# Eight blocks of a projection as one Strassen group of 512 + 512 columns, with PSUM in four pairs of banks

## The chip, the cores and the metric

The kernel runs on one core of one Trainium2 chip. The metric is the device time of one execution in microseconds, as the median of several runs; lower is better.

## What is computed

One layer of a hybrid bidirectional encoder on 512 tokens of width 2048, all in float32. The part that matters here is the input projection: h = RMSNorm(x), proj = h @ w_in, with w_in of 2048 x 10752. Its columns are cut into q, k, v and gate of a differential attention (branch A, eight heads), q, k, v and gate of a grouped-query attention with rotary positions (branch B), and two merge gates of 2048 columns.

```python
h = rmsnorm(x, norm_g)
proj = einsum('bsd,dc->bsc', h, w_in)
qa, ka, va, za, qb, kb, vb, zb, ga, gb = split(proj)
oa = diff_attention(...)                 # branch A, heads of 128
ya = (rmsnorm(oa) * 0.8 * silu(za)) @ w_out_a
ob = gqa_attention(axial_rope(rmsnorm(qb)), axial_rope(rmsnorm(kb)), vb)
yb = (ob * silu(zb)) @ w_out_b
out = rmsnorm(x + (sigmoid(ga) * ya + sigmoid(gb) * yb) @ w_o, final_g)
```

## The kernel before

**Arithmetic.** Each float32 operand of a matmul is split into a high part in fp32r (a cast on ScalarE, L103) and a low part (a subtraction on VectorE, L104). A product is three matmuls: high x high, low x high, high x low. The activations are split once; weights are split as they stream (split_w, L113), into tiles w_hi and w_lo of the pool wp, which has three buffers of each, 4 KB a partition each, and lives through the whole kernel.

**Columns and groups.** The projection is cut into blocks of 128 columns. Blocks 0, 1, 8, 9 stream plainly at the start (plain_rows). STRASSEN_BLOCKS then lists four groups of four blocks: 16 to 19, 20 to 23, 24 to 27 and 28 to 31 (in the text: groups 0 to 3). They are the values of branch A (16 to 23), keys and values of branch B (24 to 27) and queries of branch B (28 to 31). Twelve Strassen groups for the gates follow, and then the attention heads, with the rest of the projection as filler between them.

**A Strassen group (strassen, L186).** Activations are four quarters of 256 tokens x 1024 rows of the sum: a11, a12, a21, a22, and the sums s1 to s4, all held split. The weights of a group are four quarters of 1024 rows x 256 columns: b11, b12 (upper rows, left and right columns), b21, b22. Seven products of 256 x 256 x 1024 are made in the order p1 (a11 b11), p2 (a12 b21), p5 (s1), p6 (s2), p3 (s3), p4 (s4), p7 (a22). Between them VectorE makes the weight sums in place (sub, L209: b11 = b12 - b11, b11 = b22 - b11, b12 = b22 - b12, b21 = b21 - b11) and the output sums (plus, L240, and kept, L432). One product is 2 token blocks x 8 row blocks x 3 = 48 matmuls of 256 columns at L234, into one PSUM bank. For groups 0 to 3 x is the stationary operand and w moves; for the gates it is the other way round.

**Raw weights.** Eight slots w_raw of 4 KB a partition (slots, raw_tile) hold the four quarters, two slots each. After a group the list slots is rotated so that the next group takes them in the order in which they came free. Loads are issued on SP's queue.

**Results.** In group 0 the sums land in slices of xt and are stored to pv in DRAM by keep_cols, one DMA per block of 128 columns (L303). From group 1 on they land in tiles kept of the pool sp (six buffers of 2 KB) and are stored the same way.

**Pools.** Pools of tiles are opened and closed in the code; in SBUF they are stacked in the order of their opening, and a pool opened after others have closed takes their place. Over const, wraw, wp and xa (the split activations) lies xs (s1 to s4, 64 KB). Over xs lies first xn (grow 0.5 KB, xt 32 KB, two tiles early of 2 KB and some small ones), which closes after group 0, and then sp. After the gates sp and xs close, and the heads' pools at (first tile: cols) and atc (ca, sa, tables) take their place. PSUM is one pool of eight banks: four (acc) go round among the products, four (aux) are used at the start and by the heads.

**Order.** TensorE keeps the order of the program here. The instructions of VectorE, ScalarE and SP are put in order by a planner that goes by the program's order and by when an instruction can start; it also puts in the waits. Each engine then works its own list in order.

Of the kernel before, what the change touches and what calls it, by code (L numbers as in the profile page):

```python
# [11 lines left out]
F32 = mybir.dt.float32  # L12
F32R = mybir.dt.float32r
AF = mybir.ActivationFunctionType
ALU = mybir.AluOpType
AX = mybir.AxisListType

P = 128
D = 2048
S = 512  # L20
NT = S // P
NK = D // P
# [13 lines left out]
    for i in range(n)  # L36
}

STRASSEN_BLOCKS = [(16, 17, 18, 19), (20, 21, 22, 23), (24, 25, 26, 27), (28, 29, 30, 31)]
FILL_BLOCKS = [(32, 33), (2, 10), (3, 11), (34, 35), (4, 12), (5, 13), (6, 14), (7, 15)]  # L40
HEADS = "B0 B1 A0 B2 B3 B4 B5 A1 A2 B6 B7 A3 A4 A5 A6 A7".split()

# [7 lines left out]
def hybrid_block_kernel(  # L50
# [8 lines left out]
    nc = tc.nc  # L59
# [1 line left out]
    const = ctx.enter_context(tc.tile_pool(name="const", bufs=1))  # L61
    dram = ctx.enter_context(tc.tile_pool(name="dram", bufs=1, space=bass.MemoryType.DRAM))

    ps_pool = ctx.enter_context(tc.tile_pool(name="ps", bufs=1, space=bass.MemoryType.PSUM))
    banks = {}

    def share_banks(**kw):
        banks.update(kw)

    def bank(kind, shape):  # L70
        ring = banks[kind]
        ring.append(ring.pop(0))
        return ps_pool.tile([P, *shape], F32, name=kind, tag=f"bank{ring[-1]}")

    def acc_tile(*shape):
        return bank("acc", shape)
# [2 lines left out]
        return bank("aux", shape or (S,))  # L79

    wraw = ctx.enter_context(tc.tile_pool(name="wraw", bufs=1))
    wp = ctx.enter_context(tc.tile_pool(name="wp", bufs=3))

    ident = const.tile([P, P], F32, name="ident")
    make_identity(nc, ident)
# [21 lines left out]
    slots = [f"w_raw{i}" for i in range(8)]  # L107
    turn = [0]

    def raw_tile(slot, shape, dtype=F32):  # L110
        return wraw.tile([P, *shape], dtype, name="w_raw", tag=slots[slot])

    def split_w(raw, free=None):  # L113

        shape = list(raw.shape)
        if free is None:
            hi = wp.tile(shape, F32R, name="w_hi", tag="w_hi")
            lo = wp.tile(shape, F32R, name="w_lo", tag="w_lo")
        else:
            hi, lo = (raw_tile(free + i, shape[1:], F32R) for i in range(2))  # L120
        hi_lo(hi, lo, raw)
        return hi, lo
# [63 lines left out]
    def strassen(w, c_left, c_right, act, natural, tmp, done, tail=None, before={}):  # L186
# [89 lines left out]
        o = [slots[2 * i:2 * i + 2] for i in range(4)]  # L276
        slots[:] = o[1] + o[0] + o[3] + o[2]

    zg = dram.tile([2 * BW, S], F32, name="zg")
    gg = dram.tile([2 * D, S], F32, name="gg")  # L280
    og = dram.tile([2 * BW, S], F32, name="og")
# [17 lines left out]
    def keep_cols(blocks, t0, nt, v):  # L299

        for i, b in enumerate(blocks):
            written[b] = written.get(b, 0) + nt
            nc.sync.dma_start(out=pv[b, :, t0:t0 + nt, :], in_=v[:, :, i * P:(i + 1) * P])  # L303
# [21 lines left out]
    def plain_rows(blocks, place, **kw):  # L325
# [9 lines left out]

        return stream_steps(w_in, column_pieces(blocks), NK, False, act, kept, **kw)

    share_banks(acc=[0, 1, 2, 3], aux=[4, 5, 6, 7])
    with tc.tile_pool(name="xs", bufs=1) as xs:


        for n in ("s1", "s2", "s3"):
# [2 lines left out]
        with tc.tile_pool(name="xn", bufs=1) as xn:  # L345
# [106 lines left out]

            project(STRASSEN_BLOCKS[0], early, in_xt, before={"s2": late_sums})

        with tc.tile_pool(name="sp", bufs=6) as sp:
            def tmp():
                return sp.tile([P, 2, 256], F32, name="kept", tag="kept")

            for blocks in STRASSEN_BLOCKS[1:]:
                project(blocks, tmp, lambda ps: tmp())  # L460


            nc.sync.dma_start(out=sub_g, in_=subln_g.rearrange("o p -> p o"))
            nc.vector.tensor_scalar(out=sub_g, in0=sub_g, scalar1=LAM_INIT - 1.0, scalar2=None, op0=ALU.mult)
            lam4, lprod = (sp.tile([P, n, 64], F32, name="lam", tag="kept") for n in (4, 2))
            for i, v in enumerate((lq1, lk1, lq2, lk2)):
                nc.sync.dma_start(out=lam4[:, i, :], in_=v.broadcast_to([P, 64]))
            for i in range(2):
                nc.vector.tensor_tensor(out=lprod[:, i, :], in0=lam4[:, 2 * i, :], in1=lam4[:, 2 * i + 1, :], op=ALU.mult)
            nc.vector.tensor_reduce(out=lsum, in_=lprod, axis=AX.X, op=ALU.add)  # L470
            nc.scalar.activation(out=lsum, in_=lsum, func=AF.Exp)
            nc.vector.tensor_tensor(out=nlam, in0=lsum[:, 1:2], in1=lsum[:, 0:1], op=ALU.subtract)
            nc.vector.tensor_scalar(out=nlam, in0=nlam, scalar1=-LAM_INIT, scalar2=None, op0=ALU.add)


            for c0, n, func, dst in ((O_ZA, BW, AF.Silu, zg[0:BW]), (O_ZB, BW, AF.Silu, zg[BW:]),
                                     (O_GA, D, AF.Sigmoid, gg[0:D]), (O_GB, D, AF.Sigmoid, gg[D:])):
                for g in range(0, n, S):
                    def gate(th, ch, ps, sb, g=g, func=func, dst=dst):
                        v = tmp()  # L480
                        nc.vector.tensor_tensor(out=v, in0=ps, in1=sb, op=ALU.add)
                        nc.scalar.activation(out=v, in_=v, func=func)
                        row = g + ch * 256
                        nc.sync.dma_start(
                            out=dst[row:row + 256, th * 256:th * 256 + 256].rearrange("(c p) t -> p c t", p=P),
                            in_=v)

                    strassen(w_in, c0 + g, c0 + g + 256, xq, False, tmp, gate)


    share_banks(acc=[4, 5], aux=[6, 7, 0, 1, 2, 3])


# [592 lines left out]
```

## Time and profile before

| | |
|---|---|
| median of 3 runs | 1378.22 us (1376.71 to 1378.24) |
| the profiled execution | 1376.67 us |
| its span, first to last instruction | 1374.9 us |
| TensorE busy (matmuls) | 1350.2 us, 98% of the span |
| VectorE busy | 1081.1 us, 79% |
| ScalarE busy | 702.9 us, 51% |
| HBM | 144 GB/s over the span |

The predicted time is to be compared with the median; single numbers of a stage come from the profiled execution, in microseconds from the start of its span. Groups 0 to 3 run from 69.21 to 230.49, the gates after them. A matmul's end is modelled and matmuls are pipelined, so the distance between starts tells what one costs, not its duration. In the rows, L234 is the line of kernel.py, PE is TensorE, DVE VectorE, ACT ScalarE, POOL GpSimd, SP SyncE; PEld is the weight load; a q behind an engine means its queue of DMA issues.

### The profile page before, as it was taken

The numbers are of one execution on the slowest core, as the hardware profiler recorded it, in microseconds if no ns is written. First come the engines' busy times: TensorE is split into PE (matmuls) and PEld (weight loads), VectorE is DVE, ScalarE is ACT, GpSimd is POOL, SyncE is SP. The second block draws the span as 40 slices with busy tenths as digits, with TensorE's granted clock in tenths as the row PEclk, the third lists the DMA queues.
The fourth block names the chain that finished last, engine by engine and source line by source line (L and its number), as shares of the span: only waits on it lengthen the run. The fifth ranks groups of instructions, "written<-read, shape, count | busy, mean of one in ns | idle before, by whom it ended". The sixth has DMA issues, their size and how long they took to land.

```text
span 1374.9 us, 24100 instructions
## 1 busy us (share of the span) xinstructions
PE 1350.2 (98%) x9625; PEld 1274.1 (93%) x9625; DVE 1081.1 (79%) x1400; ACT 702.9 (51%) x1110; POOL 84.5 (6%) x94
## 2 busy tenths in 40 slices
PE   6999999999999999999999999999999999999997
PEld 6999999999999999999998888888788888899997
DVE  5977787777777777777759778787898858899886
ACT  7643333444444444444446675575676753354444
POOL 1000000000000000000003201000000010004322
PEclk9999999999999999999999999999999999999999
DMA  8245434543333444333377454545575446463333
GB/s 291 77 147 161 124 116 149 154 146 113 118 121 123 148 149 143 117 122 118 123 207 220 122 154 147 153 139 162 171 221 182 130 145 202 151 245 116 97 95 123
DMA packets 201743, 204.21 MB, mean 149 GB/s; under 512 B 11280, under 2 KB 175392, under 8 KB 200992
## 3 DMA queue, kind: packets, MB, share of 16 engines
q1 hardware_dynamic: 201632, 202.69, 47.5%
q8 instruction: 75, 1.23, 0.4%
q14 instruction: 36, 0.29, 0.1%
HBM read 165.68 MB, written 32.77 MB: 144 GB/s over the span
## 4 chain that ended last, share of the span: by engine, by line
PE 90%; DVE 4%; ACT 2%; DMA 1%; issue 1%; POOL 0%; SPq 0%; DVEq 0%; POOLq 0%; ACTq 0%
PE acc L234 55%; PE acc L175 27%; PE aux L621 3%; PE aux L608 2%; PE aux L739 1%; DVE w_lo L104 1%; PE aux L664 1%; PE aux L665 1%; DVE w_raw L209 1%; DMA rows<-og 1%; DMA xt<-in_x_dram 1%; PE aux L389 0%; DMA rows<-yg 0%; ACT sq L366 0%; ACT w_hi L103 0%
## 5 line engine op out<-in xcount | busy, mean ns | idle before, releaser
L103 ACT CAST w_hi<-w_raw 128x1024 fp32r<-128x1024 f32 x351 | 368.5, 1050 | 516.8 <-PE acc L234 397.9
L104 DVE TENSOR_TENSOR w_lo<-w_raw,w_hi 128x1024 fp32r<-128x1024 f32 x351 | 431.9, 1232 | 168.7 <-ACT w_hi L103 168.2
L209 DVE TENSOR_TENSOR w_raw<-w_raw 128x1024 f32<-128x1024 f32 x160 | 200.0, 1250 | 2.4
L234 PE MATMUL acc<-a2h,w_hi 128*128 128x256 f32 x384 | 108.7, 283 | 0.0
L234 PE MATMUL acc<-a2l,w_hi 128*128 128x256 f32 x384 | 108.7, 283 | 0.0
L234 PE MATMUL acc<-a2h,w_lo 128*128 128x256 f32 x384 | 108.7, 283 | 0.0
L234 PEld LDWEIGHTS acc<-a2h,w_hi 128*128 128x128 f32 x384 | 73.7, 192 | 0.0
L234 PEld LDWEIGHTS acc<-a2l,w_hi 128*128 128x128 f32 x384 | 73.7, 192 | 0.0
L234 PEld LDWEIGHTS acc<-a2h,w_lo 128*128 128x128 f32 x384 | 73.7, 192 | 0.0
L576 DVE TENSOR_REDUCE nmax<-aux 128x1 f32<-128x512 f32 x96 | 61.0, 681 | 7.5 <-PE aux L739 4.7
L175 PE MATMUL acc<-a1h,w_hi 128*128 128x512 f32 (+1 forms) x160 | 56.6, 358 | 0.2 <-ACT a1h L393 0.2
L175 PE MATMUL acc<-a1l,w_hi 128*128 128x512 f32 (+1 forms) x160 | 55.6, 353 | 0.1
L175 PE MATMUL acc<-a1h,w_lo 128*128 128x512 f32 (+1 forms) x160 | 55.7, 353 | 0.0
L175 PE MATMUL acc<-a2l,w_hi 128*128 128x512 f32 (+1 forms) x160 | 55.5, 348 | 0.0
L175 PE MATMUL acc<-a2h,w_hi 128*128 128x512 f32 (+1 forms) x160 | 55.5, 350 | 0.0
L175 PE MATMUL acc<-a2h,w_lo 128*128 128x512 f32 (+1 forms) x160 | 55.4, 347 | 0.0
L234 PE MATMUL acc<-s4h,w_lo 128*128 128x256 f32 x192 | 54.3, 283 | 0.0
L234 PE MATMUL acc<-a1h,w_hi 128*128 128x256 f32 x192 | 54.3, 283 | 0.0
L234 PE MATMUL acc<-a1l,w_hi 128*128 128x256 f32 x192 | 54.3, 283 | 0.0
L234 PE MATMUL acc<-a1h,w_lo 128*128 128x256 f32 x192 | 54.3, 283 | 0.0
L234 PE MATMUL acc<-s1h,w_hi 128*128 128x256 f32 x192 | 54.3, 283 | 0.0
L234 PE MATMUL acc<-s1l,w_hi 128*128 128x256 f32 x192 | 54.3, 283 | 0.0
(325 smaller groups left out, 4356.0 us busy)
## 6 DMA issues: line engine op xcount, KB each, us to landing
w_raw<-in_w_in_dram SPq DMA_DIRECT2D x136, 512.0 KB, 3.6
w_raw<-in_w_in_dram SPq DMA_DIRECT2D x64, 256.0 KB, 3.7
w_raw<-in_w_o_dram SPq DMA_DIRECT2D x32, 512.0 KB, 4.4
gg<-kept SPq DMA_DIRECT2D x32, 256.0 KB, 2.4
w_raw<-in_w_out_b_dram SPq DMA_DIRECT2D x32, 256.0 KB, 3.5
rows<-gg SPq DMA_DIRECT2D x32, 256.0 KB, 3.4
w_raw<-in_w_out_a_dram SPq DMA_DIRECT2D x32, 256.0 KB, 3.4
cols<-pv SPq DMA_DIRECT2D x26, 256.0 KB, 3.3
```

The source lines that it names most:

```text
L103: nc.scalar.copy(out=hi, in_=src)
L104: nc.vector.tensor_tensor(out=lo, in0=src, in1=hi.bitcast(F32), op=ALU.subtract)
L175: nc.tensor.matmul(out=acc[b][:, place], lhsT=l, rhs=r, start=first and kc == order[0] and k == 0 and i == 0, stop=last and kc == order[-1 ...
L209: nc.vector.tensor_tensor(out=d, in0=u, in1=v, op=ALU.subtract)
L234: nc.tensor.matmul(out=ps[u] if by_row else ps[:, u, :], lhsT=l, rhs=r, start=n % (2 if by_row else 4) == 0 and k == 0 and i == 0, stop=n ...
L576: nc.vector.tensor_reduce(out=nmax, in_=sps, axis=AX.X, op=ALU.max, negate=True)
L608: nc.tensor.transpose(out=tp[:, i * P:(i + 1) * P], in_=self.p[i][:, j * P:(j + 1) * P], identity=ident)
L621: nc.tensor.matmul(out=o, lhsT=l, rhs=r, start=j == 0 and i == 0, stop=j == NT - 1 and i == 2)
L664: nc.tensor.matmul(out=sp, lhsT=qs[:, sl], rhs=kh, start=True, stop=False)
L665: nc.tensor.matmul(out=sp, lhsT=qs[:, sl], rhs=kl, start=False, stop=True)
L739: nc.tensor.matmul(out=sp, lhsT=l, rhs=r, start=n == 0, stop=n == 2)
```

## The change

Groups 1 and 2 (blocks 20 to 27) become one group (WIDE_BLOCKS) in a new function strassen_wide: quarters of the weights are 1024 rows x 512 columns, products are 256 x 512 x 1024, made of 48 matmuls of 512 columns, and a product takes a pair of PSUM banks, one for each block of 128 tokens. Weights are split in pieces of one row block (128 x 512).

For this stage other pools are opened. wp is no longer a pool of the whole kernel: parts_pool opens it for the time up to group 0, then with four buffers of 2 KB for the wide stage, then with three of 4 KB for group 3 and the gates, and once more for the rest. A pool wide holds eight more raw slots of 4 KB (w_wide8 to w_wide15, for b21 and b22; b11 and b12 take the eight old slots) and one tile of 4 KB each of u, c and t. PSUM is closed and opened as four pairs of banks for the wide stage, and as eight banks again behind it (new_banks). The order of products is p1, p5, p2, p6, p3, p4, p7, and b12 is loaded ahead of b21 (late). Group 3 and the gates use strassen as before, with the list of slots put in an order that fits.

```diff
-STRASSEN_BLOCKS = [(16, 17, 18, 19), (20, 21, 22, 23), (24, 25, 26, 27), (28, 29, 30, 31)]
+STRASSEN_BLOCKS = [(16, 17, 18, 19), (28, 29, 30, 31)]
+WIDE_BLOCKS = [tuple(range(20, 28))]
...
-    ps_pool = ctx.enter_context(tc.tile_pool(name="ps", bufs=1, space=bass.MemoryType.PSUM))
+    ps_pools = ctx.enter_context(ExitStack())
     banks = {}
+    def new_banks(unit):
+        ps_pools.close()
+        banks["pool"] = unit, ps_pools.enter_context(
+            tc.tile_pool(name="ps_" + unit, bufs=1, space=bass.MemoryType.PSUM))
...
-    wp = ctx.enter_context(tc.tile_pool(name="wp", bufs=3))
+    wp = {}
+    def parts_pool(stack, bufs=3):
+        wp["pool"] = stack.enter_context(tc.tile_pool(name="wp", bufs=bufs))
...
+    wide_slots = list(range(16))
+    def strassen_wide(w, left, right, act, wide, done, late=False):
+        H = NK // 2
+        def load(q, half, pieces):
+            tiles = []
+            for p in range(4):
+                n = wide_slots[q * 4 + p]
+                r = raw_tile(n, (2, S)) if n < 8 else wide.tile([P, 2, S], F32, name="w_raw", tag=f"w_wide{n}")
+                row, at = (half * H + p * 2) * P, 0
+                for c0, n in pieces:
+                    nc.sync.dma_start(out=r[:, :, at:at + n],
+                                      in_=w[row:row + 2 * P, c0:c0 + n].rearrange("(k p) n -> p k n", p=P))
+                    at += n
+                tiles.append(r)
+            return tiles
...
+        def product(name, b):
+            ps = acc_tile(2, S)
+            ah, al = act[name]
+            for kk in range(H):
+                hi, lo = split_w(b[kk // 2][:, kk % 2, :])
+                for u in range(2):
+                    sl = slice(u * P, (u + 1) * P)
+                    for i, (l, r) in enumerate(((ah, hi), (al, hi), (ah, lo))):
+                        nc.tensor.matmul(out=ps[:, u, :], lhsT=l[:, kk, sl], rhs=r,
+                                         start=kk == 0 and i == 0, stop=kk == H - 1 and i == 2)
+            return ps
+        def tmp(tag):
+            return wide.tile([P, 2, S], F32, name="wide_" + tag, tag="wide_" + tag)
...
+        b11, b12 = load(0, 0, left), None
+        if late:
+            b12 = load(1, 0, right)
+        b21 = load(2, 1, left)
+        b12 = b12 or load(1, 0, right)
+        b22 = load(3, 1, right)
+        p1 = product("a11", b11)
+        u = tmp("u")
+        nc.scalar.copy(out=u, in_=p1)
+        if not late:
+            p2 = product("a12", b21)
+        sub(b11, b12, b11)
+        p5 = product("s1", b11)
+        if late:
+            p2 = product("a12", b21)
+        done(0, 0, plus(tmp("c"), p2, u))
+        sub(b11, b22, b11)
+        p6 = product("s2", b11)
+        plus(u, p6, u)
+        t = plus(tmp("t"), p5, u)
+        sub(b12, b22, b12)
+        p3 = product("s3", b12)
+        plus(u, p3, u)
+        done(1, 1, plus(tmp("c"), p5, u))
+        sub(b21, b21, b11)
+        done(0, 1, plus(t, product("s4", b22), t))
+        done(1, 0, plus(u, product("a22", b21), u))
...
     with tc.tile_pool(name="xs", bufs=1) as xs:
+        phase = ExitStack()
+        parts_pool(phase)
...
             project(STRASSEN_BLOCKS[0], early, in_xt, before={"s2": late_sums})
+        phase.close()
+        names = dict(enumerate(slots))
+        slots[:] = [names[i] for i in (2, 3, 0, 1, 4, 5, 6, 7)]
+        new_banks("pair")
+        share_banks(acc=[0, 1, 2, 3])
+        with tc.tile_pool(name="wide", bufs=1) as wide:
+            parts_pool(phase, 4)
+            for n, blocks in enumerate(WIDE_BLOCKS):
+                def kept(th, ch, v, blocks=blocks):
+                    keep_cols(blocks[ch * 4:ch * 4 + 4], th * 2, 2, v)
+                strassen_wide(w_in, column_pieces(blocks[:4]), column_pieces(blocks[4:]), xq, wide, kept, late=n == 0)
+            phase.close()
...
         with tc.tile_pool(name="sp", bufs=6) as sp:
+            parts_pool(phase)
+            new_banks("bank")
+            share_banks(acc=[0, 1, 2, 3], aux=[4, 5, 6, 7])
...
                     strassen(w_in, c0 + g, c0 + g + 256, xq, False, tmp, gate)
+            phase.close()
+    parts_pool(ctx)
     share_banks(acc=[4, 5], aux=[6, 7, 0, 1, 2, 3])
```

## Rows read from the trace of the kernel before

**Rows 1.** The page, part 1: engine, busy us, share, instructions

```profile
span 1374.9 us, 24100 instructions
...
PE 1350.2 (98%) x9625; PEld 1274.1 (93%) x9625; DVE 1081.1 (79%) x1400; ACT 702.9 (51%) x1110; POOL 84.5 (6%) x94
```

**Rows 2.** Chain of waits, groups 1 and 2: start us, us, what, pieces merged

```profile
109.46 80.76 PE acc L234 x673
```

**Rows 3.** Table of stages: groups 0 to 2, then a gate group

```profile
core 0: us, PE busy (x) PEld busy (x) DVE busy (x) ACT busy (x) POOL busy (x), PEclk, DMA share, GB/s
69.21:109.53 40.32, 40.32 (x338) 40.32 (x337) 29.57 (x28) 16.72 (x18) 0.00 (x0) 1.00 0.46 148
109.53:149.85 40.32, 40.32 (x338) 40.32 (x337) 30.54 (x30) 15.16 (x15) 0.00 (x0) 1.00 0.57 171
149.85:190.17 40.32, 40.32 (x338) 40.32 (x337) 30.54 (x30) 15.15 (x15) 0.00 (x0) 1.00 0.44 131
230.49:270.81 40.32, 40.32 (x338) 40.32 (x337) 31.11 (x35) 18.23 (x20) 0.00 (x0) 1.00 0.45 133
```

**Rows 4.** Timeline into group 1: start, us, instruction, [idle before <-releaser]

```profile
103.85 1.05 ACT L103 CAST w_hi<-w_raw 128x1024 fp32r<-128x1024 f32 x1 [1.83 <-PE acc L234]
...
106.73 1.05 ACT L103 CAST w_hi<-w_raw 128x1024 fp32r<-128x1024 f32 x1 [1.83 <-PE acc L234]
...
109.53 0.28 PE L234 MATMUL acc<-w_hi,a1h 128*128 128x256 f32 x1
```

**Rows 5.** Chain of waits in branch A's output projection

```profile
1129.87 68.47 PE acc L175 x302
```

**Rows 6.** Groups of TensorE instructions there: form, count, busy, mean ns, idle

```profile
L175 PE MATMUL acc<-og0h,w_lo 128*128 128x512 f32 x101 | 39.3, 389 | 0.0
L175 PE MATMUL acc<-og0l,w_hi 128*128 128x512 f32 x101 | 39.3, 389 | 0.0
L175 PE MATMUL acc<-og0h,w_hi 128*128 128x512 f32 x100 | 38.9, 389 | 0.0
```

**Rows 7.** Groups of VectorE and ScalarE instructions, 109 to 190, and 24 to 69

```profile
L104 DVE TENSOR_TENSOR w_lo<-w_raw,w_hi 128x1024 fp32r<-128x1024 f32 x29 | 35.4, 1220 | 15.0 <-ACT w_hi L103 15.0
L209 DVE TENSOR_TENSOR w_raw<-w_raw 128x1024 f32<-128x1024 f32 x16 | 19.5, 1220 | 0.3
...
L240 DVE TENSOR_TENSOR kept<-acc,kept 128x512 f32<-128x512 f32 x6 | 4.1, 692 | 2.9 <-PE acc L234 2.8
...
L103 ACT CAST w_hi<-w_raw 128x1024 fp32r<-128x1024 f32 x28 | 29.3, 1048 | 50.3 <-PE acc L234 46.7 <-DMA w_raw<-in_w_in_dram 3.7
...
L103 ACT CAST s2h<-xt 128x512 fp32r<-128x512 f32 x4 | 2.6, 642 | 0.8 <-DVE xt L407 0.8
...
L104 DVE TENSOR_TENSOR s2l<-xt,s2h 128x512 fp32r<-128x512 f32 x4 | 2.7, 682 | 0.0
```

**Rows 8.** Timeline, VectorE and SP's queue behind group 0

```profile
109.73 0.69 DVE L432 TENSOR_TENSOR xt<-acc,early 128x512 f32<-128x512 f32 x1
...
110.45 1.16 SPq L303 DMA_DIRECT2D pv<-xt  x2
...
113.48 0.35 SPq L501 DMA_DIRECT2D ca<-in_cos_a_dram  x1
```

**Rows 9.** Waits of SP's queue, 105 to 120: us in total, times, longest

```profile
SPq L501 <- DMA pv<-xt: 1.6, 2, 0.9
```

**Rows 10.** Waits of SP's queue, 710 to 721

```profile
SPq L532 <- DMA gg<-kept: 1.5, 1, 1.5
```

**Rows 11.** The stores of tile kept, 109 to 190: issue ns, time to landing

```profile
L303 SPq DMA_DIRECT2D pv<-kept x14: 360/414/470, 122.0 to 185.8; - x14
...
DMA to landing us min/median/max: 1.8/1.9/4.2
```

**Rows 12.** Table of stages around L587, TensorE alone

```profile
core 0: us, PE busy (x), PEclk, DMA share, GB/s
731.31:734.75 3.44, 1.60 (x13) 1.00 0.97 283
734.75:738.16 3.41, 3.41 (x18) 0.50 0.67 177
738.16:741.57 3.41, 3.41 (x31) 1.00 0.74 236
```

**Rows 13.** Timeline of TensorE there

```profile
733.61 1.20 PE L587 MATMUL aux<-ident,cols 128*128 128x128 f32 x8 [1.84 <-ACT w_hi L103]
...
735.21 0.41 PE L175 MATMUL acc<-w_hi,a2h 128*128 128x256 f32 x1
735.42 0.41 PE L175 MATMUL acc<-w_lo,a2h 128*128 128x256 f32 x1
```

More of the change, by code (lines that the diff above doesn't have):

```diff
@@ L72, in bank @@
         ring.append(ring.pop(0))
-        return ps_pool.tile([P, *shape], F32, name=kind, tag=f"bank{ring[-1]}")
+        unit, pool = banks["pool"]
+        return pool.tile([P, *shape], F32, name=kind, tag=f"{unit}{ring[-1]}")
     def acc_tile(*shape):
@@ L116, in split_w @@
         if free is None:
-            hi = wp.tile(shape, F32R, name="w_hi", tag="w_hi")
-            lo = wp.tile(shape, F32R, name="w_lo", tag="w_lo")
+            hi, lo = (wp["pool"].tile(shape, F32R, name=n, tag=n) for n in ("w_hi", "w_lo"))
         else:
@@ L277, in strassen, with sub, plus @@
         slots[:] = o[1] + o[0] + o[3] + o[2]
+    wide_slots = list(range(16))
[13 more added lines that the diff above has]
+            return tiles
+        def sub(dst, x0, x1):
+            for d, u, v in zip(dst, x0, x1):
+                nc.vector.tensor_tensor(out=d, in0=u, in1=v, op=ALU.subtract)
+        def product(name, b):
[11 more added lines that the diff above has]
+            return wide.tile([P, 2, S], F32, name="wide_" + tag, tag="wide_" + tag)
+        def plus(dst, ps, sb):
+            nc.vector.tensor_tensor(out=dst, in0=ps, in1=sb, op=ALU.add)
+            return dst
+        b11, b12 = load(0, 0, left), None
[25 more added lines that the diff above has]
+        done(1, 0, plus(u, product("a22", b21), u))
+        o = [wide_slots[4 * i:4 * i + 4] for i in range(4)]
+        wide_slots[:] = o[0] + o[3] + o[1] + o[2]
@@ L453, in hybrid_block_kernel @@
             project(STRASSEN_BLOCKS[0], early, in_xt, before={"s2": late_sums})
+        phase.close()
[10 more added lines that the diff above has]
+            phase.close()
+        o = [wide_slots[4 * i:4 * i + 4] for i in (0, 2, 1, 3)]
+        order = [slots[n] for q in o for n in q if n < 8]
+        slots[:] = order[0:2] + order[4:6] + order[2:4] + order[6:8]
         with tc.tile_pool(name="sp", bufs=6) as sp:
+            parts_pool(phase)
+            new_banks("bank")
+            share_banks(acc=[0, 1, 2, 3], aux=[4, 5, 6, 7])
             def tmp():
```

## Prediction

> **What bounds the kernel now.** I read the page first: TensorE is busy 98% of the span [rows 1], so time can only come out of matmuls, or be lost where TensorE waits. Then the chain of waits over the stage that the change rewrites, groups 1 and 2 (blocks 20 to 27): it is one unbroken piece of L234 matmuls, 673 in 80.76 us, 0.120 us each [rows 2]. The table of stages says the same by group: 40.32 us for 7 products of 48 matmuls, so 5.76 us a product, with VectorE busy 30.5 us and ScalarE 15.2 us of it [rows 3]. The reader is to see that nothing in this stage waits: a split of a weight half (cast to w_hi, subtract to w_lo) begins when a half is consumed and its buffer comes free. Group 1's first product starts at 109.53 and its first cast at 103.85, its second at 106.73 [rows 3, 4]. That lead of 5.7 us is what the change puts at risk.
>
> **The matmuls.** Removed: 2 x 7 x 48 = 672 matmuls of 256 columns at 0.1200 us = 80.64 us [rows 2, 3]. Added: 7 products x 8 k-blocks x 2 token blocks x 3 = 336 of 512 columns. The stage before has none of 512; the nearest is the output projection of branch A, where the chain shows 302 matmuls in 68.47 us, 0.2267 us each, all of 512 columns [rows 5, 6]. There w is the stationary operand and the activations move; here it is the other way. For 256 columns the order makes no difference: the gate group that closes the table of stages has w stationary and takes 40.32 us too [rows 3], so I take 0.2267: 336 x 0.2267 = 76.17 us. **Gain 4.5 us.** The two spacings differ by 0.1067 us for 256 columns, so each matmul has 0.0133 us that doesn't scale with columns, and 336 of these vanish: the same 4.5 us.
>
> The Trainium skill has a rule against this: "TensorE: Matmul & The Clock Gate", section "Back-to-back issue gap", puts the warm gap at columns/2.4 + 2.5 ns, which would save 336 x 2.5 ns, an estimate of 0.8 us, and the sum below would be 3.7 us higher. The measured spacings give 13.3 ns in place of 2.5, so the trace disagrees and the rows decide.
>
> **ScalarE and VectorE in the wide stage.** Bytes split are unchanged, pieces are half as long: 56 casts of 512 columns at 0.65 us plus one copy = 37 us against 28 at 1.05 plus two copies = 31 us; VectorE 56 x 0.68 + 16 subtractions x 1.22 + 7 sums of 1024 columns at 1.22 to 1.38 (one as long as the SBUF form, or two of 0.69) = 67 us against 61 [rows 3, 7]. That is 88% of 76 us in place of 76% of 80.6, hidden under matmuls as long as the split stays ahead. Three buffers of 2.88 us let a cast start 5.8 us before its use, of which 3.5 remain after cast and w_lo; four of 1.36 us let it start 4.1 us before, and 2.8 remain. Two output sums in a row, 2.5 us, still fit. I cost it at 0, bound 0 to 2 us: groups 1 and 2 lose nothing with subtractions and sums among their splits [rows 2]. Loads stay 16 x 512 KB, stores 16 x 128 KB: 0. PSUM: products go round four pairs as they went round four banks: 0 inside the stage.
>
> **The seams, where I expect the change to be decided.** Before, the split buffers (w_hi, w_lo) were one pool for the whole kernel. Now that pool is closed and opened anew ahead of the wide stage, behind it, and after the gates. What does a pool opened over closed ones wait for? The trace answers twice. Tables ca and the others, whose pool lies partly over the closed xn, were issued at 113.48, after the last of xt's stores, and the wait view gives that store as the releaser [rows 8, 9]; and the first load of the heads' pool (cols) waited for a gate store out of sp [rows 10], though by the order of the pools it lies where s1 was, which the products had finished with by then. So I take the whole closed pool as what is waited for, its stores included.
>
> Seam 1. From the code's sizes: over xs lay wp (24 KB), then xn (xt 32 KB, early 4 KB and small tiles). wide is 8 raw tiles + u, c, t of 4 KB = 44 KB, and the new wp of 16 KB lies on it, at 44 to 60 KB: over xn, which ran from 24 to about 61. The first split of the wide stage thus waits until group 0's last result has left xt. TensorE runs dry at 109.53; the sum is at 109.73, its two stores go at 110.45 and have landed by 113.4 [rows 8]. Then a cast of 0.65 to 114.1, two matmuls, and the third needs w_lo, another 0.68, at about 114.8, where it would have been at 109.53 + 2 x 0.227 = 110.0. **Stall 4.9 us** (4.3 if the second store goes at once; 7 if loads of b21 and b22, queued on SP behind the same release, or other transfers slow the stores, whose landings run from 1.8 to 4.2 us [rows 11]). Behind the waiting cast on ScalarE stand only the later casts, behind w_lo on VectorE the later splits and subtractions; only TensorE waits for them. b21 and b22 are used two products later, 22 us away: hidden.
>
> Seam 2. sp (12 KB) and the next wp (24 KB) lie over wide, 0 to 36 KB of 44. The first split of group 28 to 31 waits for the wide stage's last result u: sum of 1024 columns from 0.2 us after TensorE ran dry, 1.25 us long, four stores 0.41 to 0.47 us apart, the last going at 2.8 and landing 1.9 later, at 4.7 [rows 7, 8, 11]; wake 0.2, cast of 1024 1.05, w_lo 1.22: the third matmul at 7.4 in place of 0.24. **Stall 7.2 us** (6.5 if the stores overlap better; 9.5 if landings take the 4.2 us). The loads for this group are free to run two products earlier, so the queue should be quiet.
>
> Seam 3, gates to heads: the new wp lies over xs alone, last read by the p4 matmuls of the last group, 5.76 us before the fill starts; two splits fit. Nothing, bound 0 to 1 us. The reopened PSUM pools wait by the same rule for the last sums that read the old banks, done 0.9 us (seam 1) and 1.5 us (seam 2) after TensorE ran dry: inside the stalls, nothing more.
>
> Clock. TensorE's one long wait after the start, 1.84 us before L587, was followed by 3.41 us at a granted clock of 0.50, the 1.2 GHz level, with matmuls 0.213 us apart in place of 0.120 [rows 12, 13]. Half of 3.41 us is lost: 1.7 us. Both stalls are longer, so I charge it at each: **3.4 us**, from 0 (it does not fall) to 6.8 (twice as long at the lower level each time).
>
> **Sum.** -4.5 + 4.9 + 7.2 + 3.4 = +11.0 us on the profiled execution's 1376.67 (span 1374.9 and 1.8 around it): 1387.7. The median of the three runs is 1378.22, 1.5 higher, and gives 1389.2; I state 1388.5, between them.
>
> **Rivals.** (a) The other side: the new split buffers find nothing pending below them, so splits run ahead through both seams and only the matmuls count. Price: 1376.67 - 4.5 to 1378.22 - 4.5 = 1372.2 to 1373.7. For it: before, every group boundary passes without a gap [rows 2]. Against: the sizes put both wp pools over pools whose last act is a store. It decides below a total stall of 4.5 us, about 2.2 us a seam; the landing of the stores alone exceeds that. 0.07. (b) Waits bind, the clock stays up: 1376.67 + 7.6 to 1378.22 + 7.6 = 1384.3 to 1385.8. Against: 1.84 us sufficed once. 0.12. (c) The change doesn't do what it says: columns alone set the price, the gain is 0 and the stalls remain, 1376.67 + 15.5 to 1378.22 + 15.5 = 1392.2 to 1393.7. Against: the two spacings [rows 2, 5]. 0.04. By the gap that the Trainium skill states (page and section above) it would be 1391.4 to 1392.9, close to this case. (d) In the wide stage VectorE, at 88%, lets the shorter lead run out; two sums and a subtraction in a row, 3.7 us, overrun the 2.8 us that the lead leaves; at one miss of 1 us per product, 1394.7 to 1396.2. Against: each subtraction needs only the casts of its own tile, so they can be spread, and groups 1 and 2 run without a miss [rows 2]. 0.07. (e) Forecast, 0.70.
>
> **How the numbers follow.** Range 1382 to 1394: the low end is -4.5 with stalls of 4.3 + 6.5 and no clock loss on the profiled execution (1383), and 1 us for stores that land faster than any row shows; the high end takes stalls of 7 + 8, the clock loss and the 2 us of the wide stage (1392.6 to 1394.1). It leaves out (a) and the far end of (d). A run of this kernel can tell 0.2%, 2.8 us, from no change. (a) and nothing else is faster: 0.06 with 0.01 of it within 0.2%; (b) with both stalls at a third of their size adds 0.03 within; the rest is slower: 0.90.
>
> **What would show it.** Right: matmuls of the wide stage 0.227 us apart; idle of 4 to 5 us on TensorE ahead of the first of them and of 6 to 8 us behind the last, ended by a ScalarE cast that itself waited for a pv store; a granted clock of 0.50 behind each; the rest of the kernel shifted by a constant. Wrong: casts of the first wide half before group 0's last matmul; a spacing of 0.24; TensorE waits inside the wide stage on w_lo; a loss elsewhere.

## The result, and the profile after

The changed kernel takes 1394.03 us (median, 1393.31 to 1394.48); the kernel before took 1377.47 beside it (1375.69 to 1378.24). The ratio is 1.0122, 95% interval 1.0104 to 1.0139: slower, by 16.6 us between the medians, where +11.0 was forecast. The time lies at the upper edge of the range of 1382 to 1394, just outside it. The profiled execution took 1394.41 us, 17.7 more than that of the kernel before.

The page, part 1 (engine, busy us, share, instructions), to be set beside [rows 1]:

```profile
span 1392.5 us, 23508 instructions
...
PE 1352.1 (97%) x9289; PEld 1260.5 (91%) x9289; DVE 1080.7 (78%) x1421; ACT 708.1 (51%) x1137; POOL 85.4 (6%) x94
```

There are 336 fewer matmuls, and the span is 17.6 us longer. Where it went is told by the waits of TensorE, here those between 100 and 260 us (us in total, times, longest); in the kernel before the list is empty there, and [rows 2] is its chain:

```profile
PE acc L245 <- ACT w_hi L115: 6.1, 1, 6.1
PE acc L324 <- ACT w_hi L115: 4.6, 1, 4.6
PE acc L324 <- DVE wide_c L332: 3.1, 1, 3.1
PE acc L245 <- DVE w_lo L116: 0.5, 1, 0.5
```

The second is the seam ahead of the wide group, the first the seam behind it; both were forecast. The third is not in the prediction. The chain of waits over the same stretch (start us, us, what; the pieces that matter) has all of them in their order:

```profile
109.97 0.70 DVE xt L523
...
111.48 2.12 DMA pv<-xt
...
113.85 0.63 ACT w_hi L115
...
114.52 57.22 PE acc L324 x240
171.77 0.49 DVE wide_u L332
...
173.60 1.15 DVE wide_c L332
...
174.88 23.49 PE acc L324 x96
198.39 1.24 DVE wide_u L332
...
201.10 1.96 DMA pv<-wide_u
...
203.31 1.05 ACT w_hi L115
204.39 1.24 DVE w_lo L116
...
205.67 44.40 PE acc L245 x357
```

In [rows 2] this was one piece of matmuls. Now the first matmul of p1 (114.52) follows a sum into xt, its store and a cast, as the prediction had it; five products on (240 matmuls) TensorE stops again, for two sums of VectorE and a w_lo between them, before it makes p4 and p7 (96 matmuls); then it waits for a sum, four stores and the split of the next group.

The table of stages with one line for each product p1, p5, p2, p6, p3, p4, p7 (TensorE alone; it answers to [rows 3]):

```profile
core 0: us, PE busy (x), PEclk, DMA share, GB/s
114.52:128.05 13.53, 13.53 (x48) 0.80 0.86 310
128.05:138.93 10.88, 10.88 (x49) 1.00 0.01 2
138.93:149.81 10.88, 10.88 (x49) 1.00 0.01 2
149.81:160.69 10.88, 10.88 (x49) 1.00 0.81 245
160.69:171.73 11.04, 11.04 (x49) 1.00 0.61 186
174.88:187.31 12.43, 12.43 (x48) 0.88 0.15 42
187.31:198.35 11.04, 11.04 (x49) 1.00 0.18 49
```

An undisturbed product is 10.88 us, 48 matmuls of 0.2267: the size that the prediction took from [rows 5]. (The lines of 11.04 reach to the modelled end of the last matmul, those of 10.88 to the start of the next product.) p1 and p4 are 2.65 and 1.55 us longer, and they are the ones with a granted clock below 1. The stretches behind the three waits (the answer to [rows 12], with the columns of [rows 3]):

```profile
114.52:119.91 5.39, 5.39 (x13) 4.18 (x14) 5.36 (x7) 2.42 (x5) 0.00 (x0) 0.50 0.93 325
174.88:177.93 3.05, 3.05 (x7) 2.44 (x8) 0.00 (x0) 0.55 (x1) 0.00 (x0) 0.50 0.62 172
204.41:208.66 4.25, 3.79 (x16) 3.49 (x17) 4.25 (x4) 1.84 (x2) 0.00 (x0) 0.50 0.99 294
```

The granted clock was at 0.50 for longer than these lines, since it fell while TensorE was still waiting ahead of p1 and behind the wide group. The whole stretches (TensorE alone, columns as in the table by product):

```profile
113.08:119.91 6.83, 5.39 (x13) 0.50 0.74 257
201.83:208.65 6.82, 3.78 (x16) 0.50 0.74 217
```

What they cost is half of the time under matmuls, 5.39 and 3.78 us: 2.7 and 1.9 us. The part that fell into a wait cost nothing.

The budget against the kernel before, each from starts of products: group 0 to p1 and through it +7.4 (4.59 of wait, 2.65 in p1, the rest in the first step), p4 +4.9 (3.14 + 1.55, the rest its own first steps), behind the wide group +8.6 (6.05 of wait, and about 2.4 in the first product of blocks 28 to 31: 0.46 for the first w_lo, 1.9 for the clock), matmuls -4.5. That is +16.4 by the start of the gates. Of what comes later, 1.3 is one place: ahead of the heads' first transposes TensorE waits 3.14 us (L702) in place of the 1.84 at L587 [rows 13]:

```profile
PE aux L702 <- issue: 3.1, 1, 3.1
```

Together +17.7; the spans differ by 17.6.

Why p4 waits: VectorE's timeline there (start, us, instruction, [idle before <-releaser]):

```profile
171.77 1.23 DVE L332 TENSOR_TENSOR wide_u<-acc,wide_u 128x1024 f32<-128x1024 f32 x1 [0.24 <-PE acc L324]
172.91 0.68 DVE L116 TENSOR_TENSOR w_lo<-w_raw,w_hi 128x512 fp32r<-128x512 f32 x1
173.51 1.22 DVE L332 TENSOR_TENSOR wide_c<-acc,wide_u 128x1024 f32<-128x1024 f32 x1
```

The last of them is c = p5 + u, the result (1, 1), which reads p5 in PSUM. The four pairs form a ring, taken in turn by the products in their order p1, p5, p2, p6, p3, p4, p7, so p4 gets the pair of the second product. In the kernel before the second product is p2, whose last reader, the result (0, 0), is made right behind it. Here (late order) it is p5, whose last reader needs u after p3, the product immediately ahead of p4. The experiments test this reading, and the rest of the budget.

### The profile page after: what moved, and what is told of

The parts are those of the page before. It is cut to its first block, busy times and chain, and to the rows that moved or that the text cites. A ratio compares the mean times of both kernels' runs of the same rounds, so it can differ in the third digit from the quotient of the medians.

```text
span 1392.5 us, 23508 instructions
## 1 busy us (share of the span) xinstructions
PE 1352.1 (97%) x9289; PEld 1260.5 (91%) x9289; DVE 1080.7 (78%) x1421; ACT 708.1 (51%) x1137; POOL 85.4 (6%) x94
## 4 chain that ended last, share of the span: by engine, by line
PE 91%; DVE 4%; ACT 2%; DMA 2%; issue 1%; POOL 0%; SPq 0%; DVEq 0%; POOLq 0%; ACTq 0%
PE acc L245 50%; PE acc L186 26%; PE acc L324 6%; PE aux L736 3%; PE aux L723 2%; PE aux L854 1%; DVE w_lo L116 1%; PE aux L779 1%; PE aux L780 1%; DMA rows<-og 1%; DMA xt<-in_x_dram 1%; PE aux L480 0%; ACT w_hi L115 0%; PE aux L702 0%; ACT sq L457 0%
## 5 line engine op out<-in xcount | busy, mean ns | idle before, releaser
L115 ACT CAST w_hi<-w_raw 128x1024 fp32r<-128x1024 f32 (+1 forms) x379 | 373.5, 987 | 523.2 <-PE acc L245 343.3
L116 DVE TENSOR_TENSOR w_lo<-w_raw,w_hi 128x1024 fp32r<-128x1024 f32 (+1 forms) x379 | 434.7, 1151 | 177.7 <-ACT w_hi L115 177.2
L220 DVE TENSOR_TENSOR w_raw<-w_raw 128x1024 f32<-128x1024 f32 x144 | 180.4, 1254 | 2.0
L245 PE MATMUL acc<-s1h,w_lo 128*128 128x256 f32 x192 | 54.3, 283 | 0.0
```

The source lines that it names most:

```text
L115: nc.scalar.copy(out=hi, in_=src)
L116: nc.vector.tensor_tensor(out=lo, in0=src, in1=hi.bitcast(F32), op=ALU.subtract)
L220: nc.vector.tensor_tensor(out=d, in0=u, in1=v, op=ALU.subtract)
L245: nc.tensor.matmul(out=ps[u] if by_row else ps[:, u, :], lhsT=l, rhs=r, start=n % (2 if by_row else 4) == 0 and k == 0 and i == 0, stop=n ...
```

## The experiments

**e1_ring: p4 takes another pair.**

```diff
         sub(b21, b21, b11)
+        acc = banks["acc"]
+        acc[0], acc[1] = acc[1], acc[0]
         done(0, 1, plus(t, product("s4", b22), t))
```

> The changed kernel with one thing different: ahead of the product p4 the ring of PSUM pairs is turned, so that p4 takes the pair of p2 and p7 the pair of p5. Theory (the 3.1 us that TensorE waits ahead of p4 are a wait for the pair: p5 is read last by the sum that also needs p3): TensorE runs from p3 into p4 without a wait, the 3.41 us at a granted clock of 0.50 behind it are gone too, and the span falls by about 4.9 us, from 1392.5 to 1387.6; ratio to the kernel before 1.0086. Rival (p4 comes late because VectorE is late with the split of its weights or with its sums, and the pair only ends last): the wait stays at about 3 us with another releaser, span 1392 to 1393, ratio 1.012. Either way both seams keep their stalls of 4.6 and 6.1 us.

Measured: ratio 1.0094 (1.0078 to 1.0109), 3.9 us less than the change; span of the profiled execution 1389.2. The waits of TensorE between 100 and 260 us, and then the chain's piece for the wide group:

```profile
PE acc L245 <- ACT w_hi L115: 6.0, 1, 6.0
PE acc L324 <- ACT w_hi L115: 4.5, 1, 4.5
PE acc L245 <- DVE w_lo L116: 0.5, 1, 0.5
```

```profile
114.54 79.16 PE acc L324 x336
```

All seven products are one piece; the wait on wide_c is gone, and so is the half-clock stretch behind it. The wide group ends at 193.69 in place of 198.35: 4.7 us earlier. VectorE's work is the same, so it was the pair and not VectorE's load. The span gave back 3.3 us in the profiled execution, the longest of four (1387.2 to 1389.2). Half of the missing 1.4 us went at the seam behind the wide group, where more of the half-clock stretch lay under matmuls (5.46 us in place of 3.78), the rest behind 700 us.

**e2_order: the other order in the code.** The call is made with `late` false: p1, p2, p5, with b21 loaded ahead of b12.

> The changed kernel with the other order that its code holds: p1, p2, p5 in place of p1, p5, p2, with b21 loaded behind b11. By the ring p4 then takes the pair of p2, read last by the sum made right behind p2. Theory (pair of p5): the wait ahead of p4 is gone, as with the turned ring, and p7, which now takes p5's pair, starts 10.9 us later, when the sum has long been made: span down by 4.9 us to about 1387.6, if b21 arrives before p2 needs it at 125.4; its loads go at about 114 to 116 and should land by 122. Rival (VectorE is late): the wait ahead of p4 stays, span 1392 to 1393. A third outcome: b21 comes late and TensorE waits ahead of p2, by 1 to 3 us, so that the order with p5 first was needed; span 1388 to 1391 with a wait that a load ends.

Measured: ratio 1.0088 (1.0073 to 1.0103), span 1387.0. The chain's piece:

```profile
114.66 77.81 PE acc L324 x336
```

No wait inside the group, ahead of p2 either: b21 is there in time. So it is the late order that costs the 4.9 us by way of the ring, and the loads do not need it. The piece is 1.35 us shorter than in e1_ring, because the half-clock stretch behind seam 1 was 3.41 us here and 6.83 there.

**e3_seam2: results apart from what the next pools lie over.** u, c and t are taken from a pool of their own, opened behind the split buffers; behind the wide group the split buffers are opened first and the kept tiles (sp) on top of them.

```diff
+            sums = phase.enter_context(tc.tile_pool(name="sums", bufs=1))
...
-        with tc.tile_pool(name="sp", bufs=6) as sp:
+        with ExitStack() as phase:
             parts_pool(phase)
+            sp = phase.enter_context(tc.tile_pool(name="sp", bufs=6))
```

> The changed kernel with u, c and t in a pool of their own behind the split buffers, so that what is opened behind the wide group (first the split buffers, then the kept tiles) lies over the raw tiles and the old split buffers alone, and over no tile that is stored. PSUM is opened anew as before. Theory (the pool is waited for as a whole, stores included): the first cast of blocks 28 to 31 no longer waits for the four stores of the last result; what is left is the matmuls that read the old split buffers last and the last sum out of PSUM, done 1.4 us behind the last wide product. The stall behind the wide group falls from 6.1 us to 1.4 to 2.5 us; with the clock loss (none to 1.7 us, and 0.5 for the first w_lo) the span falls by 3 to 6 us, to 1387 to 1389.5, ratio 1.009 to 1.010. Rival (loads of blocks 28 to 31, or PSUM, end last): the stall stays at 5 to 6 us. Seam 1 and the wait ahead of p4 stay as they are.

Measured: ratio 1.0073 (1.0056 to 1.0090), 6.7 us less than the change, more than expected. What is left of the wait and the stretch behind it, in the table of stages (TensorE alone, columns as in the table by product):

```profile
198.53:200.10 1.57, 0.00 (x2) 1.00 0.00 0
200.10:203.51 3.41, 3.41 (x28) 1.00 0.55 154
```

The stores are out of the chain, and the clock stayed at 1.00, so the whole 8.6 us shrank to about 1.6. The profile names no releaser for the 1.57 us that are left; they end 0.1 us after the last sum out of PSUM (198.78 to 200.00). (The profiled execution, span 1388.2, is the longest of four, the others had 1384.8 to 1385.6; it has a stretch at 0.50 among the heads, at 1007.6, that no other trace of this case has.)

**e4_seam1: split buffers apart from xt.**

```diff
+        parts_pool(phase, 4)
         with tc.tile_pool(name="wide", bufs=1) as wide:
-            parts_pool(phase, 4)
...
-            phase.close()
+        phase.close()
```

> The changed kernel with the split buffers of the wide phase opened ahead of the pool of raw tiles, so that they lie over the old split buffers alone and not over the tile that group 0's results are stored from. Theory: the first cast of the wide group waits only for the last matmul of group 0, which read the old split buffers last, and p1 for the sum out of PSUM, 0.9 us: the stall ahead of p1 falls from 4.6 to 1 to 1.5 us, and with the half-clock stretch shorter or gone (up to 1.7 us) the span falls by 3.5 to 6 us, to 1386.5 to 1389, ratio 1.008 to 1.0095. Rival (the wait is for the loads of b11, or for PSUM): the stall stays at about 4.6 us. A point that it decides besides: whether a stall of 1 to 1.5 us is followed by a stretch at a granted clock of 0.50. The wait ahead of p4 and the seam behind the wide group stay as they are.

Measured: ratio 1.0085 (1.0070 to 1.0100), 5.1 us less than the change; span 1384.8. The cast and the first matmul in the timeline, and then the table of stages for the wait and the stretch behind it:

```profile
109.89 1.66 ACT L115 CAST w_hi<-w_raw 128x512 fp32r<-128x512 f32 x3 [7.71 <-PE acc L245]
...
110.72 0.47 PE L324 MATMUL acc<-w_hi,a1h 128*128 128x512 f32 x1 [0.88 <-DVE xt L523]
```

```profile
109.85:110.72 0.87, 0.00 (x0) 1.00 0.00 0
110.72:114.13 3.41, 3.41 (x14) 1.00 0.27 79
```

The cast now waits for the last matmul of group 0 and no longer for a store, and the matmul for the last sum out of the old PSUM pool: 0.88 us, with the clock at 1.00 behind it. The profiled execution is the shortest of four (spans 1384.8 to 1388.5), and its 7.7 us are not all the repair's: the wait ahead of p4 is still there, but the clock stayed up behind it, which saves the 1.5 us that p4 lost in the change.

```profile
165.53:168.67 3.14, 0.00 (x1) 1.00 0.00 0
168.67:172.08 3.41, 3.41 (x15) 1.00 0.55 154
```

**e7_pools: the seams without the wide group.** The kernel before, groups of 256 + 256, with only the pool of split buffers closed and opened anew: ahead of group 1 (over 36 KB for the kept tiles of groups 1 and 2), behind group 2 and after the gates.

```diff
+        phase.close()
+        with tc.tile_pool(name="wide", bufs=1) as wide:
+            parts_pool(phase)
...
+            phase.close()
         with tc.tile_pool(name="sp", bufs=6) as sp:
+            parts_pool(phase)
...
+            phase.close()
+    parts_pool(ctx)
```

> The kernel before, its groups 0 to 3 of 256 + 256 columns and its PSUM banks unchanged, with only the split buffers closed and opened anew where the change does it: ahead of blocks 20 to 27 over the tile that group 0's results are stored from, behind them over the pool of kept tiles, and after the gates. It measures the seams without the wide products. Theory (a pool waits for all of the closed pool below it, stores included): a stall of 4.5 to 5 us ahead of group 1, ended by a ScalarE cast that waited for the store of group 0's last result; one of 3.5 to 4.5 us behind group 2 (a sum of 512 columns, 0.7 us, and two stores in place of a sum of 1024 and four); 3.4 us lost to the clock behind the first and 1.7 to 3.4 behind the second; 1 us more ahead of the heads: +14 us, ratio 1.009 to 1.011. Rival (the stalls come from the wide products, their loads or their PSUM pairs): no stall over 1 us, ratio 1.000 to 1.001.

Measured: ratio 1.0145 (1.0131 to 1.0159), +20 us, above the expected +14. Its chain between 109 and 250 us:

```profile
111.48 2.01 DMA pv<-xt
...
113.74 1.05 ACT w_hi L107
...
116.10 83.05 PE acc L237 x670
199.17 0.70 DVE kept L437
...
200.81 3.41 DMA sa<-in_sin_a_dram
```

The last line names the load of a table, which landed as the first cast ended (204.2). What held that cast is in ScalarE's timeline:

```profile
203.15 2.94 ACT L107 CAST w_hi<-w_raw 128x1024 fp32r<-128x1024 f32 x3 [11.69 <-DMA pv<-kept]
```

The seams need no wide products: 4.92 us of wait ahead of group 1, 5.11 behind group 2 (3.5 to 4.5 was expected; the two stores took 2.5 us each to land beside loads of tables, against 1.9 in [rows 11]), 6.83 us at a granted clock of 0.50 at each, 6.23 and 5.58 of them under matmuls, and 3.50 us ahead of the heads. By the trace this is 4.9 + 5.1 + 0.9 (two waits for w_lo) + 5.9 (half of 11.8) + 1.7 (at the heads) = 18.5 us; the spans differ by 19.4, and the rest was not followed up.

**e9_heads: the third seam alone.** The kernel before, with the split buffers opened inside xs, behind the activations, and closed and opened once, ahead of the heads.

> The kernel before with only the third seam of the change: the split buffers are one pool from the start to the last gate, lying behind the activations, and are closed and opened anew once, ahead of the heads, over the place of s1. It asks whether this seam is what makes TensorE wait 2.4 to 3.5 us ahead of the heads' first transposes in the changed kernel and its variants, in place of 1.84 us. Theory (the first split of the fill waits for the last matmuls of the gates, and the loads behind it delay the store and the load that the transposes wait for): that wait is 3 to 3.5 us here too, followed by 3.41 us at a granted clock of 0.50 as before; span 1 to 2 us above the kernel before, ratio 1.0005 to 1.0015. Rival (this wait moves by a microsecond with any shift of the stage ahead, as in the fitted kernel with halves, where no pool is opened anew and it was 2.85 us): 1.5 to 2.9 us, ratio 0.999 to 1.0005.

Measured: ratio 1.0013 (1.0004 to 1.0022), +1.8 us; the wait ahead of the transposes:

```profile
PE aux L595 <- issue: 3.3, 1, 3.3
```

As in the change (3.1), and 1.8 in the kernel before. So the third seam has a price, 0.6 to 3 us by the times. How it comes about is not settled: the issue of the heads' first load waits 4.0 us for the last gate store here and 3.9 in the change, against 1.5 in the kernel before, as the theory has it; but the wait ahead of the transposes was 1.53 us in e5_fitted and 2.85 in e6_halves, below, neither of which opens a pool anew, so the rival has a part in it.

**e5_fitted: the wide group with split buffers and PSUM never closed.** From the kernel before: the pools of split buffers and of PSUM banks are left as they were, splits stay whole raw tiles (128 x 1024), a product is two tiles of one bank, b21's weight sum is made early so that b11's raw tiles can hold c and t, and p4 takes the banks of p2.

```diff
+            ps = [acc_tile(S) for _ in range(2)]
+            ah, al = act[name]
+            for p in range(4):
+                hi, lo = split_w(b[p])
...
+        p6 = product("s2", b11)
+        sub(b21, b21, b11)
+        plus(u, p6, u)
+        t, c11, c00 = b11[0], b11[1], b11[2]
...
+        acc = banks["acc"]
+        acc[:4] = acc[2:4] + acc[:2]
+        p4 = product("s4", b22)
```

> The kernel before with the wide group of 512 + 512 columns put in so that no pool is closed ahead of TensorE: split buffers and the eight PSUM banks stay one pool each for the whole kernel, a split is a whole raw tile of 128 x 1024 as before, a product is two tiles of one bank each and its sums two of 512 columns, c and t lie in raw tiles of b11 that are read no more, and p4 takes the banks of p2. Theory (the matmul gain is real, 336 x 0.0133 = 4.5 us, and all else that the change lost is waits for pools and for the pair of p5): no wait at the seams, products of 10.88 us, and the time falls to 4.5 us below the kernel before, 1372.7 us, ratio 0.9967 (0.996 to 0.998). Rival (the seams are the price of wide products whatever the pools do, since the sums, stores and splits of a product twice as long must end somewhere): stalls of some us stay in 95 to 260 us and the ratio is 1.000 to 1.008.

Measured: 1370.95 us against 1375.25, ratio 0.9967 (0.9955 to 0.9980). Between 95 and 720 us the list of TensorE's waits is empty; the chain and then the table of stages over the wide group (columns as in [rows 3]):

```profile
110.00 76.19 PE acc L316 x336
```

```profile
109.84:186.03 76.19, 76.19 (x339) 63.09 (x337) 60.07 (x59) 31.61 (x33) 0.00 (x0) 1.00 0.42 135
```

So the wide group is worth what its matmuls say, 80.64 - 76.19 = 4.45 us, and this version beats both kernels. The prediction's rival (a), in which only the matmuls count, is thus a kernel that exists, with other pools.

**e6_halves: the same with each 512-column matmul as two of 256.**

```diff
+                            for c in (slice(0, 256), slice(256, 512)):
+                                nc.tensor.matmul(out=ps[u][:, c], lhsT=l[:, kk, sl], rhs=r[:, k, c],
...
```

> The fitted kernel (one pool of split buffers, one of banks) with every matmul of 512 moving columns of the wide group issued as two of 256: 672 matmuls in place of 336 on the same data. It measures the gain of the matmuls alone. Theory (each matmul has 0.0133 us that does not scale with its columns): 0.1200 us apart, 11.52 us a product in place of 10.88, span 4.5 us above the fitted kernel, about the time of the kernel before, ratio 0.9995 to 1.0005. Rival (columns alone set the price, or the second half costs less since the same weights are loaded again): 0.113 to 0.117 us apart, span 0 to 2.5 us above the fitted kernel, ratio 0.997 to 0.9985.

Measured: ratio 1.0007 (0.9998 to 1.0016). The chain over the group, and the table of stages (columns as in [rows 3]):

```profile
109.65 80.64 PE acc L317 x672
```

```profile
109.65:190.29 80.64, 80.64 (x674) 80.64 (x674) 60.49 (x59) 31.53 (x33) 0.00 (x0) 1.00 0.40 128
```

To the hundredth the 80.64 of the kernel before (0.1200 us each), though every second matmul has the weights of the one ahead of it. But each has a weight load of its own all the same, 674 of each in this stretch. So the price that does not scale with columns is per matmul with its weight load; which of the two has it was not tested. (The medians differ by 5.5 us and not 4.45; in the profiled executions the wait ahead of the heads was 2.85 us here, with 3.41 us at 0.50 behind it, and 1.53 in e5_fitted, with none.)

**e8_all: the three repairs in the changed kernel.** e1_ring, e3_seam2 and e4_seam1 together; pools are still closed and opened.

> The changed kernel with the three repairs together, its pools still closed and opened: the ring turned ahead of p4, the split buffers of the wide phase over the old ones alone, and u, c and t apart from what lies under the next pools. Theory (the three causes are apart and add up): 0.9 us of wait ahead of p1, none ahead of p4, 1.6 us behind the wide group, no stretch at a granted clock of 0.50 between 95 and 260 us; from 1392.5 the span falls by 6.5 + 4.9 + 7 to about 1374, and the time is within 2 us of the kernel before: ratio 0.998 to 1.001. Against the fitted kernel it keeps the 0.9 + 1.6 us for the last sum out of PSUM and about 1 us ahead of the heads. Rival (a repair only lets the stall show at the next seam): ratio 1.003 to 1.007.

Measured: ratio 1.0029 (1.0017 to 1.0041), 1378.93 us: above the theory's range and just under the rival's, which the interval reaches. The profiled execution has the mechanism of the theory, waits of 0.9 and 1.4 us and 0.6 for a w_lo, no stretch at 0.50 there, and a span of 1375.6. These waits and the 1.6 us more ahead of the heads (3.5 in place of 1.8) add up to 4.5 us, as much as the wide matmuls give. But it is the shortest of six executions; the others have spans of 1376.7 to 1379.2, and the mean granted clock over the six is 0.996, against 0.998 for the kernel before. 0.002 of 1376 us is some 2.5 us, most of what is missing. That these executions lost their clock at the short waits of the seams would fit, but is not shown: only the shortest has a trace.

## Why the prediction was wrong, point by point

**The step that failed** is "PSUM: products go round four pairs as they went round four banks: 0 inside the stage". It was said of the number of banks and not of who reads them. The order p1, p5, p2 gives p4 the pair of p5, and there TensorE waited 3.14 us and lost 1.55 to the clock behind it, 4.9 us with p4's first steps where 0 stood. e1_ring, which changes the pair alone, and e2_order, which changes the order of products and loads, take the wait away. The price could have been had from the same rows: after p3 come a sum of 1024 columns, a w_lo and another sum, 1.22 + 0.68 + 1.22 = 3.1 us [rows 7], and half of 3.41 us for the clock, 1.7. With those 4.8 us the sum is +15.8 and the statement 1393.3. The bound of 0 to 2 us for ScalarE and VectorE did not cover it, as it was a bound on splits coming late, and rival (d) had the two sums in a row but let them starve splits.

**The matmuls: right.** -4.5 us forecast, -4.45 in e5_fitted against e6_halves; operand order makes no difference at 512 columns either (0.2268 us each in e5_fitted with x stationary, 0.2267 in [rows 5] with w). The Trainium skill, page "TensorE: Matmul & The Clock Gate", section "Back-to-back issue gap", would have made it an estimate of 0.8 us by its formula for the isolated gap; the runs decide against it.

**Splits in the wide stage: right.** From 128.05 to 171.73 TensorE does not wait, with pieces of 512 columns in four buffers; rival (d) falls.

**Seam 1: mechanism right, size short.** The cast waited for xt's store and the first matmul came 4.59 us late (4.9 with w_lo was forecast); but the clock was at 0.50 for 6.83 us and not 3.41, and 5.39 of these lay under matmuls. Together 7.4 where 4.9 + 1.7 = 6.6 stood. e4_seam1 shows the cause.

**Seam 2: right.** 8.6 us where 7.2 + 1.7 = 8.9 stood: the last store took 1.96 us and the idle time was 6.05 + 0.46; the clock was low for twice as long as charged, but 3.0 of the 6.82 us lay in idle time, so it cost 1.9. That is a stall 0.5 shorter and a clock 0.2 dearer than forecast. e3_seam2 shows the cause.

**Seam 3: forecast at 0, bound 0 to 1.** It is 1.3 us in the trace and 1.8 (0.6 to 3.0) by e9_heads; how it comes about is open.

**Clock: right in kind, short in size.** It fell at both seams as charged (rival (b) falls), but for 6.83 us at each, 2.7 and 1.9 us lost under matmuls where 1.7 stood each time, and a third time behind p4, which was not in the sum.

**The sum.** 11.0 forecast, 17.7 measured on the profiled execution: 4.9 (p4) + 0.8 (seam 1) + 1.3 (ahead of the heads) - 0.3 (seam 2) = 6.7, the whole difference. The sign and its reason, seams that cost more than the matmuls give, held.

## What to carry to other kernels

When the order of products changes, write down for each PSUM buffer of the ring its last reader and what that reader waits for: a ring as long as before can put a product onto a buffer whose last reader depends on the product just ahead. A pool that was closed and opened anew on a saturated engine's path made its first tile wait here for the last store out of the pool that it then lay over (4.6 and 6.1 us; 4.9 and 5.1 in e7_pools), and no longer when it lay over no stored tile; keep the pool and put short-lived tiles into dead ones, or lay the new pool over tiles that are not stored. Price a wait of TensorE together with the matmul time that may run at the lower clock behind it.

## What the runs showed of the hardware

**The clock behind a wait.** In the traces of this case, after waits of 0.88, 1.36, 1.53 and 1.57 us (e4_seam1, e8_all, e5_fitted, e3_seam2) the granted clock stayed at 1.00; after 1.84 to 3.5 us (kernel before, ahead of p4 and of the heads) it went to 0.50, the 1.2 GHz level, for 3.41 us, but not behind the 3.14 us ahead of p4 in e4_seam1, where it stayed at 1.00; after 4.5 to 6.1 us for 6.83 us, but once (e2_order, 4.66 us) for 3.41. Short waits are not safe, though: in e3_seam2 0.94 and 0.63 us among the heads were followed by 3.41 us at 0.50. So the length of a wait alone does not tell what follows it. A wait of 4.59 us cost 7.4 in all, and one of 6.05 shortened to 1.57 us gave back 7.0.

**The second half of a matmul pair with the same weights** costs as much as the first when each has its own weight load: 0.1200 us each in e6_halves.
